# A pair's first product is copied to a second PSUM bank by ScalarE, and TensorE adds the second product there

## The chip, the cores and the metric

The kernel runs on one core of a Trainium2 chip. The metric is the device time of one execution in microseconds (us); a kernel is run several times, and the median is given. The hardware profiler records one execution, whose instructions make up the profile. TensorE does the matrix products into PSUM, a memory of eight banks of 128 x 512 fp32 numbers; VectorE and ScalarE read the banks and write to SBUF, the working memory; GpSimd (POOL) and SyncE (SP) mostly issue transfers here.

## The reference

Two layers of a block with two branches, on 512 tokens of width 1024, in fp32:

```python
h = rmsnorm(x, norm1_g[i])
z = h @ w_in[i] + b_in[i]              # q,k,v,o, gates of both branches
hm = mlstm_chunkwise(...)              # branch A, 4 heads, q and k through a causal conv
hr = retention_chunkwise(...)          # branch B, 4 heads
merged = sigmoid(gm) * (y_m @ w_bm[i]) + sigmoid(gr) * (y_r @ w_br[i])
x = x + merged @ w_out[i]
h2 = rmsnorm(x, norm2_g[i])
x = x + square(relu(h2 @ w_ff1[i] + b_ff1[i])) @ w_ff2[i] + b_ff2[i]
h3 = rmsnorm(x, norm3_g[i])
x = x + sigmoid(h3 @ w_pe_gate[i]) * (p[i] @ w_pe[i])
return rmsnorm(x, final_g)             # after both layers
```

The weights are square matrices of width 1024 or strips of it; the feed-forward is 4096 wide.

## The kernel before

**Precision.** A product in fp32 is made of three products of a shorter type: each operand is split into a high part, copied by ScalarE (L309), and a low part, the difference, made by VectorE (L310). TensorE then multiplies high by high, high by low and low by high into one bank. The weights are split as they arrive, into buffers that hold three blocks of each sort: w, w_A, w_B, w_C, w_D, w_t. A block of 128 x 1024 takes one instruction of each engine.

**Pairs.** A part of the products is made in units called PAIR, by a scheme of seven half-size products in place of eight (`run_pair`, L520). Each of the seven, P1 to P7, is 12 matmuls of 128 x 256: four row blocks by three precision terms. TensorE does them in the order P1, P5, then the P4 that the previous pair has left (`flush`), P6, P2, P3, P7. A pair uses three banks: P1, P6, P7 and P4 are summed in bank a, one on top of the other; P5 and P3 in bank c; P2 is alone in bank b. After every product a reader takes out what stands in its bank, and the next product on the same bank waits for that reader. So P6 waits for the reader of P1, P7 for that of P6, and P4 for that of P7. There are 75 pairs, 35 in the first layer and 40 in the second.

**Readers.** In `pair_tiles` (L597), used for the projections, the gates and the pairs of the first feed-forward product, ScalarE copies P1 out (L612) and VectorE adds P2 to it (L616). In `ff2` (L1524), the second feed-forward product (32 of the 75 pairs, tiles named l0o00 to l1o33), VectorE adds each product to x (L1530 where it is the first to touch x, L1532 elsewhere); there P1 and P2 go to the same quarter of x.

**What sets the order.** The program is written in one sequence, and a scheduler sorts the instructions of each engine from it by readiness and priority; the readers of `pair_tiles` are raised (`tc.high_priority(AHEAD)`). At run time each engine goes through its list in order and waits where something is not ready. A bank comes from a pool, `ps`, of eight; a tile that asks for one waits for the last reader of the tile that had it.

**The first head.** In the mLSTM the four column blocks of q and k (l0m0z0 to z3, `mm3`, L488 to L490) and the four token blocks of v (l0m0vp0 to vp3, L809 to L811) are made ahead of the norm's factor, which VectorE multiplies in when it reads z (L1040); z0 is the first that it reads. In the list before, TensorE takes vp0 to vp3 in turn for each block of weights.

Of the kernel before, what the change touches and what calls it, by code (L numbers as in the profile page):

```python
# [35 lines left out]
F32 = mybir.dt.float32  # L36
F32R = mybir.dt.float32r
AF = mybir.ActivationFunctionType
OP = mybir.AluOpType
# [3 lines left out]
P = 128  # L43
T = 512
# [7 lines left out]
S = 256  # L52
UN = 1024
LOOK = 2
AHEAD = 250
WARM = 13
# [23 lines left out]
def ff_order():  # L80

    seq = [("f", 0, p) for p in range(4)]
    for b in range(3):
        seq.append(("f", b + 1, 0))
        seq += [("o", b, p) for p in range(4)]
        seq += [("f", b + 1, p) for p in range(1, 4)]
    return seq, [("o", 3, p) for p in range(4)]
# [166 lines left out]
def build(ctx, tc, ins, out):  # L254
    nc = tc.nc
    ve, ac, gp, te = nc.vector, nc.scalar, nc.gpsimd, nc.tensor
# [3 lines left out]
    def pool(name, bufs, **kw):  # L260
        return ctx.enter_context(tc.tile_pool(name=name, bufs=bufs, **kw))
# [8 lines left out]
    wpool = pool("w", PIECES)  # L270
    bpool = pool("big", 1)
    opool = pool("one", 1)
    psum = pool("ps", 8, space=bass.MemoryType.PSUM)
    cur = {}

    xs_dram = tc.dram_tile([KT, P, T], F32, name="x_spill")
# [20 lines left out]
    ones = ones_r.bitcast(F32)  # L297
# [3 lines left out]

    def ps(name):
        return psum.tile([P, T], F32, name=name, tag="ps")

    def tmp(name, dt=F32):
        return cur["tmp"].tile([P, T], dt, name=name, tag="t", bufs=cur["ntmp"])
# [64 lines left out]
    def pace():  # L371
        if at["step"] < len(steps) and at["credit"] >= 0:
            step()
# [6 lines left out]
    def next_unit():  # L380
        n = at["unit"]
        at["unit"] += 1
        tick("FULL" if full(n) and units[n][0] == "PAIR" else units[n][0])
        return n
# [92 lines left out]
    def ready(k):  # L477
        while at["prep"] < min(len(order), k + 1):
            prep_next()

    def unit(kind):
        n = next_unit()
        assert units[n][0] == kind, (units[n], kind)
        ready(place[n, 0] + LOOK)
        return units[n], *pieces.pop((n, 0))
# [6 lines left out]
    def t8(act, name):  # L492

        _, wh, wl = unit("T8")
        o = ps(name)
        for k in range(KT):
            s = slice(k * P, (k + 1) * P)
            mm3(o, wh[:, s], wl[:, s], act[0][k], act[1][k], k == 0, k == KT - 1)
            if k == 3:
                flush()  # L500
            if k in (2, 5):
                pace()
        return o

    def acts(pl, name):
        hi, lo = [], []
        for k in range(KT):
            hi.append(pl.tile([P, T], F32R, name=f"{name}h{k}", tag="ah", bufs=KT))
            lo.append(pl.tile([P, T], F32R, name=f"{name}l{k}", tag="al", bufs=KT))
        return hi, lo  # L510
# [4 lines left out]
    def flush():  # L515

        while later:
            later.pop()()

    def run_pair(name, act, done):  # L520

        n = next_unit()
        assert units[n][0] == "PAIR", units[n]
        bank = {}

        def product(x):
            w, half, j = PRODUCTS[x]
            ready(place[n, "A"] + READY[x])
            wh, wl = [a[:, half * Q:(half + 1) * Q] for a in pieces[n, w]]
            b = {"P2": "b", "P5": "c", "P3": "c"}.get(x, "a")  # L530
            first = x in ("P1", "P2", "P5")
            if first:
                bank[b] = ps(f"{name}{b}")
            o = bank[b][:, 0:S]
            for k in range(4):
                s = slice(k * P, (k + 1) * P)
                h, l = act[k](j)
                f, e = first and k == 0, k == 3
                te.matmul(o, wh[:, s], h, start=f, stop=False, skip_group_check=True)
                te.matmul(o, wh[:, s], l, start=False, stop=False, skip_group_check=True)  # L540
                cur["mm"] = te.matmul(o, wl[:, s], h, start=False, stop=e, skip_group_check=True)  # L541
            done(x, o)
            pace()

        def last():
            product("P4")
            for w in PIECE:
                del pieces[n, w]

        product("P1")  # L550
        product("P5")
        flush()
        for x in ("P6", "P2", "P3", "P7"):
            product(x)
        later.append(last)
# [34 lines left out]
                then[x, u]()  # L590
            pace()

    def ahead():

        return tc.high_priority(AHEAD)

    def pair_tiles(name, act, consume, y=None, then=None):  # L597

        y = y or [tmp(f"{name}y{d}") for d in range(2)]
        a, b = slice(0, S), slice(S, T)  # L600

        def done(x, o):
            with ahead():
                evict(x, o)
            if then and x in then:
                then[x]()
            if x == "P4":
                consume(y)

        def evict(x, o):  # L610
            if x == "P1":
                ac.activation(y[0][:, b], o, AF.Copy)  # L612
            elif x == "P5":
                ac.activation(y[1][:, a], o, AF.Copy)
            elif x == "P2":
                ve.tensor_tensor(y[0][:, b], o, y[0][:, b], OP.add)  # L616
            elif x == "P6":
                ac.activation(y[1][:, b], o, AF.Copy)
            elif x == "P3":
                ve.tensor_tensor(y[1][:, b], o, y[1][:, b], OP.add)  # L620
            elif x == "P7":
                ve.tensor_tensor(y[1][:, a], o, y[1][:, a], OP.add)
            else:
                ac.activation(y[0][:, a], o, AF.Copy)

        run_pair(name, act, done)
# [142 lines left out]
    def bcol(i, n, k):  # L769
        o, _ = _B[n]  # L770
        return bvec(i, o + k)
# [187 lines left out]
    def big(name, dt):  # L959

        return [bpool.tile([P, T], dt, name=f"{name}{k}", tag="big", bufs=KT) for k in range(KT)]

    x = big("x0", F32)
# [2 lines left out]
    cur["tmp"], cur["ntmp"] = cur["low"], NTMP  # L966
    cur["room"] = range(room)
    n1 = Norm("l0n1", 0, "g1", acts(xa_pool, "l0n1"))
    warm = ps("warm")
    for _ in range(WARM):  # L970
        te.matmul(warm[:, 0:P], ones, ones, start=True, stop=True)
    nc.sync.dma_start(x[0], ins["xT"][0])
    fill_raws(2)
    nc.scalar.dma_start(bc[:, 0, 8:NK], ins["vecs"][0][:, 8:NK])
# [11 lines left out]
    for i in range(L):  # L986
# [34 lines left out]
        _, wi = unit("IF")  # L1021
        _, wh, wl = unit("T8")
        og = ps(f"l{i}if")
        oz = ps(f"l{i}m0z0")
        for k in range(KT):
            s = slice(k * P, (k + 1) * P)
            f, e = k == 0, k == KT - 1
# [281 lines left out]
        for d in range(4):  # L1309
            o = t8(xa, f"l{i}m0z{d}") if d else oz  # L1310
# [115 lines left out]
        for c in range(KT):  # L1426
# [6 lines left out]
            o = t8(yr, f"l{i}br1{c}")  # L1433
# [13 lines left out]
        if i == L - 1:  # L1447
            x_pool = phase("x", act_side)
            whole = x_pool.tile([P, KT, T], F32, name=f"l{i}x", tag="x")
            x = [whole[:, c, :] for c in range(KT)]  # L1450
        else:
            x = big(f"l{i}x", F32)
# [18 lines left out]
        for c in range(KT):  # L1471
            o = t8((mh, ml), f"l{i}wo{c}")
# [47 lines left out]
        def tile3(c):  # L1520
            n3.tile(c, x[c])

        def ff2(b, p):
            started = set()  # L1524

            def add(q, o, op):
                y = x[2 * p + q // 2][:, (q % 2) * S:(q % 2 + 1) * S]
                if b == 0 and q not in started:
                    started.add(q)
                    ve.scalar_tensor_tensor(y, y, bcol(i, "bf2", 2 * p + q // 2), o, OP.add, op)  # L1530
                else:
                    ve.tensor_tensor(y, y, o, op)  # L1532

            def done(x_, o):
                if x_ in ("P1", "P2"):
                    add(1, o, OP.add)
                elif x_ == "P5":
                    add(2, o, OP.subtract)
                elif x_ in ("P6", "P3"):
                    add(3, o, OP.subtract)  # L1540
                elif x_ == "P7":
                    add(2, o, OP.subtract)
                elif x_ == "P4":
                    add(0, o, OP.add)
                    if b == 3 and p == 3:
                        tile3(6)
                        tile3(7)
                if b == 3 and p and x_ in ("P6", "P7"):
                    tile3(2 * p - 2 + (x_ == "P7"))

            def parts(k):
                h, l = hid[b, k]
                return lambda j: (h[:, j * S:(j + 1) * S], l[:, j * S:(j + 1) * S])

            run_pair(f"l{i}o{b}{p}", [parts(k) for k in range(4)], done)

        first, rest = ff_order()
# [59 lines left out]
        for c in range(KT - LAST if last else KT):  # L1617
            o = t8(n3.act, f"l{i}pg{c}")
# [44 lines left out]
    for a, n in enumerate(nn):  # L1663
        for c in range(KT - LAST, KT):
            _, wh, wl = ws[c - KT + LAST]
            o = ps(f"pl{a}{c}")[:, :256]
# [141 lines left out]
```

## Time and profile before

| | |
|---|---|
| median of 3 runs | 2288.41 us (2288.2 to 2289.22) |
| the profiled execution | 2288.05 us |
| its span | 2286.3 us |
| matmuls | 13532 |
| TensorE busy | 2266.4 us |
| VectorE busy | 1761.6 us in 2722 instructions |
| ScalarE busy | 1265.9 us in 1835 instructions |
| granted TensorE clock | 0.998 |

Names in rows give the tile written, an arrow, and the tiles read. "L310 DVE" is an instruction of line 310 on VectorE, ACT is ScalarE, PE is TensorE. A timeline row gives the start in us from the span's start, the duration, and in brackets the idle time before it and who ended it. Tile numbers are left out: l0m0z stands for z0 to z3.

### The profile page before, as it was taken

What the parts mean: (1) busy time and instruction counts of PE and PEld (TensorE: products, weight loads), DVE (VectorE), ACT (ScalarE), POOL (GpSimd) and SP (SyncE); (2) the same over time, 40 slices, a digit from 0 to 9 for tenths busy, and PEclk for the clock granted to TensorE, in tenths of its full rate; (3) what the DMA queues carried; (4) which work ended last, traced back from release to release, by engine and by line L of the source; (5) the groups of instructions that cost most, each with busy time, mean ns of one, the idle gap of its engine ahead of it and who ended that gap; (6) DMA issues with size and microseconds to landing.
All of it is one profiled execution on the core that took longest, in us unless ns stands there. A gap on an engine that the chain in (4) does not pass through costs nothing.

```text
span 2286.3 us, 36395 instructions
## 1 busy us (share of the span) xinstructions
PE 2266.4 (99%) x13532; PEld 2011.6 (88%) x13532; DVE 1761.6 (77%) x2722; ACT 1265.9 (55%) x1835; POOL 610.0 (27%) x952
## 2 busy tenths in 40 slices
PE   9999999999999999999999999999999999999998
PEld 8888899888898899999888888988888888999997
DVE  7877777886677878778778787778867678787785
ACT  6766544654554546556557564445545446566564
POOL 3332222223124322223532332221231242111112
PEclk9999999999999999999999999999999999999999
DMA  6776887787789888888886768877876888888841
GB/s 214 191 193 175 245 231 220 217 234 213 230 239 267 218 229 233 236 247 221 219 224 182 197 179 249 238 215 225 227 221 213 247 265 218 248 235 229 233 162 56
DMA packets 187890, 499.33 MB, mean 218 GB/s; under 512 B 26352, under 2 KB 29808, under 8 KB 187712
## 3 DMA queue, kind: packets, MB, share of 16 engines
q0 software_dynamic: 57520, 188.53, 36.9%
q1 hardware_dynamic: 114496, 280.97, 36.3%
q10 hardware_dynamic: 15696, 27.50, 3.5%
q8 instruction: 106, 1.74, 0.3%
q14 instruction: 72, 0.59, 0.1%
HBM read 478.03 MB, written 194.51 MB: 294 GB/s over the span
## 4 chain that ended last, share of the span: by engine, by line
PE 87%; DVE 7%; ACT 2%; issue 2%; DMA 2%; POOL 0%; SPq 0%; DVEq 0%; ACTq 0%; POOLq 0%
PE l1br L488 1%; PE l0br L489 1%; PE l0br L488 1%; PE l1br L489 1%; PE l0br L490 1%; PE l1br L490 1%; PE l0f L488 1%; PE l0f L490 1%; PE l0f L489 1%; DVE w_B L310 1%; DVE w_C L310 1%; PE l1f L488 1%; PE l0pg L488 1%; PE l1f L490 1%; PE l1bm L488 1%
## 5 line engine op out<-in xcount | busy, mean ns | idle before, releaser
L309 ACT ACTIVATE w<-wr 128x1024 fp32r<-128x1024 f32 (+1 forms) x193 | 199.7, 1041 | 124.7 <-issue 28.5
L310 DVE TENSOR_TENSOR w<-wr,w 128x1024 fp32r<-128x1024 f32 (+1 forms) x193 | 234.1, 1216 | 43.7 <-ACT w L309 42.8
L309 ACT ACTIVATE w_B<-wr 128x1024 fp32r<-128x1024 f32 x123 | 130.4, 1060 | 148.8 <-PE l1bm L490 13.1
L310 DVE TENSOR_TENSOR w_B<-wr,w_B 128x1024 fp32r<-128x1024 f32 x123 | 150.2, 1222 | 54.3 <-ACT w_B L309 53.8
L309 ACT ACTIVATE w_C<-wr 128x1024 fp32r<-128x1024 f32 x75 | 79.3, 1058 | 65.0 <-issue 6.8
L310 DVE TENSOR_TENSOR w_C<-wr,w_C 128x1024 fp32r<-128x1024 f32 x75 | 92.5, 1233 | 25.6 <-ACT w_C L309 24.7
L310 DVE TENSOR_TENSOR w_A<-wr,w_A 128x1024 fp32r<-128x1024 f32 x75 | 91.7, 1223 | 13.7 <-ACT w_A L309 9.6
L309 ACT ACTIVATE w_A<-wr 128x1024 fp32r<-128x1024 f32 x75 | 79.1, 1054 | 41.2 <-DMA wr<-wpairs 4.4
L309 ACT ACTIVATE w_t<-wr 128x1024 fp32r<-128x1024 f32 x56 | 59.4, 1060 | 64.1 <-PE l1g2va L585 6.3
L309 ACT ACTIVATE w_D<-wr 128x512 fp32r<-128x512 f32 x75 | 47.3, 631 | 81.8 <-DVE wr L470 27.4
L310 DVE TENSOR_TENSOR w_t<-wr,w_t 128x1024 fp32r<-128x1024 f32 x56 | 68.3, 1222 | 21.3 <-ACT w_t L309 20.7
L488 PE MATMUL l0f<-l0n2h,w 128*128 128x512 f32 x176 | 68.7, 390 | 0.0
L489 PE MATMUL l0f<-l0n2l,w 128*128 128x512 f32 x176 | 68.6, 390 | 0.0
L490 PE MATMUL l0f<-l0n2h,w 128*128 128x512 f32 x176 | 68.5, 389 | 0.0
L310 DVE TENSOR_TENSOR w_D<-wr,w_D 128x512 fp32r<-128x512 f32 x75 | 51.7, 690 | 15.0 <-ACT w_D L309 14.5
L367 POOL DMA_DIRECT2D s30t<-wpairs x24 | 16.8, 701 | 92.3 <-PE l1o10a L541 9.2
L490 PEld LDWEIGHTS l0f<-l0n2h,w 128*128 128x128 f32 x176 | 33.0, 188 | 7.0
L488 PEld LDWEIGHTS l0f<-l0n2h,w 128*128 128x128 f32 x176 | 33.0, 188 | 6.6
L489 PEld LDWEIGHTS l0f<-l0n2l,w 128*128 128x128 f32 x176 | 33.0, 188 | 6.5
L488 PE MATMUL l1f<-l1n2h,w 128*128 128x512 f32 x96 | 37.6, 391 | 0.0
L489 PE MATMUL l1f<-l1n2l,w 128*128 128x512 f32 x96 | 37.4, 390 | 0.0
L490 PE MATMUL l1f<-l1n2h,w 128*128 128x512 f32 x96 | 37.4, 389 | 0.0
(5796 smaller groups left out, 9080.3 us busy)
## 6 DMA issues: line engine op xcount, KB each, us to landing
wr<-wstream SPq DMA_DIRECT2D x189, 512.0 KB, 4.8
wr<-wpairs SPq DMA_DIRECT2D x225, 256.0 KB, 4.0
wr<-wwide SPq DMA_DIRECT2D x48, 512.0 KB, 4.5
s3t<-wwide POOLq DMA_DIRECT2D x24, 256.0 KB, 4.7
s6t<-wwide POOLq DMA_DIRECT2D x24, 256.0 KB, 5.2
s18t<-wwide POOLq DMA_DIRECT2D x24, 256.0 KB, 5.5
s21t<-wwide POOLq DMA_DIRECT2D x24, 256.0 KB, 5.0
s24t<-wpairs POOLq DMA_DIRECT2D x24, 256.0 KB, 6.3
```

The source lines that it names most:

```text
L309: a = ac.activation(hi_ap, src, AF.Copy)
L310: return a, ve.tensor_sub(lo_ap, src, hi_ap.bitcast(F32))
L367: dma = gp.dma_start(piece(g, x, p, q), piece(g, MADE[x][a], p, q), max_dma_last_dim=4096, **kw)
L488: te.matmul(o, sh, mh, start=first, stop=False)
L489: te.matmul(o, sh, ml, start=False, stop=False)
L490: cur["mm"] = te.matmul(o, sl, mh, start=False, stop=last)
```

## The change

Each pair keeps its three banks, but b now comes from a pool of its own with one bank, `psb`, and the common pool `ps` has seven. When P1 is done, ScalarE copies bank a into bank b. P2 is then started without clearing, so that TensorE adds it onto the copy, and P2's reader takes out the sum: in `pair_tiles` a copy of ScalarE where VectorE's addition was, in `ff2` one addition to x where there were two. So a pair has one addition of VectorE less and one copy of ScalarE more; the number of matmuls is the same. The matmuls of the warm-up at the program's start write to the two halves of what P2 uses of the new bank, whose accumulation marks are set by that; no later matmul clears them.

```diff
-    psum = pool("ps", 8, space=bass.MemoryType.PSUM)
+    psum = pool("ps", 7, space=bass.MemoryType.PSUM)
+    psum_b = pool("psb", 1, space=bass.MemoryType.PSUM)
...
+    def seeded(name):
+
+        return psum_b.tile([P, T], F32, name=name, tag="psb")
...
     def run_pair(name, act, done):
...
-            first = x in ("P1", "P2", "P5")
+            first = x in ("P1", "P5")
             if first:
                 bank[b] = ps(f"{name}{b}")
...
-            done(x, o)
+            if x == "P1":
+                bank["b"] = seeded(f"{name}b")
+                with ahead():
+                    ac.activation(bank["b"][:, 0:S], o, AF.Copy)
+            else:
+                done(x, o)
             pace()
...
         def evict(x, o):
-            if x == "P1":
+            if x == "P2":
                 ac.activation(y[0][:, b], o, AF.Copy)
             elif x == "P5":
                 ac.activation(y[1][:, a], o, AF.Copy)
-            elif x == "P2":
-                ve.tensor_tensor(y[0][:, b], o, y[0][:, b], OP.add)
...
-    warm = ps("warm")
-    for _ in range(WARM):
-        te.matmul(warm[:, 0:P], ones, ones, start=True, stop=True)
+    warm = seeded("warm")
+    for k in range(WARM):
+        te.matmul(warm[:, k % 2 * P:k % 2 * P + P], ones, ones, start=k == 0, stop=True, skip_group_check=True)
...
             def done(x_, o):
-                if x_ in ("P1", "P2"):
+                if x_ == "P2":
                     add(1, o, OP.add)
```

The scheduler sorts the lists anew, so that instructions also stand elsewhere far from the pairs. Three places follow; line numbers of the changed kernel are five to eight higher.

TensorE at the first head of the first layer, before (vp2 and vp3 are the third and fourth token block of v; w5 is the first block of weights, w7 the third):

```order
L810 MATMUL l0m0vp2_618<-w5_0_447,l0n1h0_202 128x512
L811 MATMUL l0m0vp2_618<-w5_0_447,l0n1l0_203 128x512
L809 MATMUL l0m0vp3_619<-w5_0_447,l0n1h0_202 128x512
L810 MATMUL l0m0vp3_619<-w5_0_447,l0n1h0_202 128x512
L811 MATMUL l0m0vp3_619<-w5_0_447,l0n1l0_203 128x512
L809 MATMUL l0m0vp0_616<-w5_0_447,l0n1h1_204 128x512
```

and of the change, where vp3's first matmul stands:

```order
L817 MATMUL l0m0vp2_621<-w7_0_626,l0n1h4_213 128x512
L818 MATMUL l0m0vp2_621<-w7_0_626,l0n1h4_213 128x512
L819 MATMUL l0m0vp2_621<-w7_0_626,l0n1l4_214 128x512
L817 MATMUL l0m0vp3_622<-w5_0_450,l0n1h0_205 128x512
L818 MATMUL l0m0vp3_622<-w5_0_450,l0n1h0_205 128x512
L819 MATMUL l0m0vp3_622<-w5_0_450,l0n1l0_206 128x512
```

vp3 now begins only when vp0 to vp2 have gone through five of their eight row blocks: 45 matmuls behind vp0's first, where it was 9. In the second layer it is 50.

VectorE at the same place, before (l0gf to l0gc are the gates' rows, w_0 a block of weights that is split, l0m00z the read of z0):

```order
L913 SCALAR_TENSOR_TENSOR l0gf<-l0gf,l0gd 4x512
L310 TENSOR_TENSOR w_0_655<-wr_406,w_0_655 128x1024
L919 SCALAR_TENSOR_TENSOR l0glb<-ones_r,l0glf 4x128 x4
L921 SCALAR_TENSOR_TENSOR l0gm<-l0glf,l0gli 4x512
L937 TENSOR_TENSOR l0gc<-l0gli,l0glb 4x128
L923 TENSOR_TENSOR l0gr__522<-l0glb,l0gm 4x512
L937 TENSOR_TENSOR l0gc<-l0gli,l0glb 4x128 x3
L1040 TENSOR_TENSOR l0m00z<-l0m0z_317,l0n1rb 128x512
```

and of the change:

```order
L921 SCALAR_TENSOR_TENSOR l0gf<-l0gf,l0gd 4x512
L927 SCALAR_TENSOR_TENSOR l0glb<-ones_r,l0glf 4x128 x4
L929 SCALAR_TENSOR_TENSOR l0gm<-l0glf,l0gli 4x512
L945 TENSOR_TENSOR l0gc<-l0gli,l0glb 4x128
L931 TENSOR_TENSOR l0gr__525<-l0glb,l0gm 4x512
L945 TENSOR_TENSOR l0gc<-l0gli,l0glb 4x128 x3
L1048 TENSOR_TENSOR l0m00z<-l0m0z_320,l0n1rb 128x512
```

The split of a block of weights, one instruction, no longer stands ahead of the read of z0.

VectorE at the pair l0o10 of the second feed-forward product, before (l0o10a is the pair's bank a, the row with it is P1's addition):

```order
L1494 TENSOR_TENSOR l0f20st<-l0f_8929,l0n2rb 128x512
L310 TENSOR_TENSOR w_B<-wr_8838,w_B 128x1024
L1532 TENSOR_TENSOR l0x_7205<-l0x_7205,l0o10a 128x256
L631 TENSOR_TENSOR l0f20st<-l0f20st 128x512
L470 TENSOR_TENSOR wr_8838<-wr_8838 128x512
```

of the change, the same place on VectorE:

```order
L1502 TENSOR_TENSOR l0f20st<-l0f_8932,l0n2rb 128x512
L315 TENSOR_TENSOR w_B<-wr_8841,w_B 128x1024
L475 TENSOR_TENSOR wr_8841<-wr_8841 128x512
L639 TENSOR_TENSOR l0f20st<-l0f20st 128x512
L315 TENSOR_TENSOR l0hl_8861<-l0f20st,l0hh_8860 128x768
```

and on ScalarE, where L554 is the new copy of bank a to bank b:

```order
L314 ACTIVATE w_B<-wr_8841 128x1024
L554 ACTIVATE l0o10b<-l0o10a 128x256
L1503 ACTIVATE l0f20st<-l0f20st,bc 128x512
L1504 ACTIVATE l0f20st<-l0f20st 128x512
```

P1's addition is gone from VectorE, and the copy stands on ScalarE directly behind the high half of w_B.

More of the change, by code (lines that the diff above doesn't have):

```diff
@@ L518, in flush, with ahead @@
             later.pop()()
+    def ahead():
+        return tc.high_priority(AHEAD)
     def run_pair(name, act, done):
@@ L591, in run_wide @@
             pace()
-    def ahead():
-        return tc.high_priority(AHEAD)
     def pair_tiles(name, act, consume, y=None, then=None):
```

## The prediction

> **What bounds the kernel now.** I read the page first, then the waits of TensorE, then single sites in the timeline.
>
> ```profile
> span 2286.3 us, 36395 instructions
> PE 2266.4 (99%) x13532; PEld 2011.6 (88%) x13532; DVE 1761.6 (77%) x2722; ACT 1265.9 (55%) x1835; POOL 610.0 (27%) x952
> PE 87%; DVE 7%; ACT 2%; issue 2%; DMA 2%; POOL 0%; SPq 0%; DVEq 0%; ACTq 0%; POOLq 0%
> ```
>
> The span is TensorE's own work: it is busy 99%, and the chain that ended last lies on it for 87%. VectorE's 77% is cover as long as its result comes before TensorE asks for it. The number of matmuls doesn't change, so at best the change takes from the 2286.3 - 2266.4 = 19.9 us that TensorE idled. The next view says who ended that idle time; the columns are the wait, its releaser, us in total, times and longest. These are the rows inside the pairs.
>
> ```profile
> PE l1o20a L539 <- DVE l1x L1532: 1.2, 1, 1.2
> PE l1f10a L541 <- DVE w_B L310: 0.8, 1, 0.8
> PE l0o10a L539 <- DVE l0x L1532: 0.7, 1, 0.7
> PE l0o20a L539 <- DVE l0x L1532: 0.7, 1, 0.7
> PE l1o10a L540 <- DVE l1hl L310: 0.6, 1, 0.6
> PE l1o32a L539 <- DVE l1x L1532: 0.5, 1, 0.5
> PE l1o00a L539 <- DVE l1x L1532: 0.5, 1, 0.5
> ...
> PE l1o10a L539 <- ACT l1hh L309: 0.4, 1, 0.4
> ...
> PE l1o20a L540 <- DVE l1hl L310: 0.3, 1, 0.3
> PE l0o30a L541 <- DVE w_B L310: 0.3, 1, 0.3
> PE l1o30a L541 <- DVE w_B L310: 0.3, 1, 0.3
> PE l1o33a L539 <- DVE l1x L1532: 0.3, 1, 0.3
> PE l1bgm2a L541 <- DVE w_B L310: 0.3, 1, 0.3
> PE l0bgm2a L541 <- DVE w_B L310: 0.3, 1, 0.3
> ...
> PE l1f10a L539 <- ACT l1f10st L612: 0.2, 1, 0.2
> PE l1o10b L541 <- DVE w_B L310: 0.2, 1, 0.2
> PE l1o20b L541 <- DVE w_B L310: 0.2, 1, 0.2
> PE l0o00a L539 <- DVE l0x L1530: 0.2, 1, 0.2
> ```
>
> Eighteen waits. Seven are on an addition of VectorE that empties a bank (1.2 + 0.7 + 0.7 + 0.5 + 0.5 + 0.3 + 0.2 = 4.1 us), eleven on a weight or operand that is split late, or in one case copied out late by ScalarE (0.8 + 0.6 + 0.4, five of 0.3 and three of 0.2: 3.9 us). Together 8.0 us, 0.35% of the span. No row names a bank outside the pairs: with eight banks nothing waits for one.
>
> What one costs in full is seen at the first product P6 of l0o10.
>
> ```profile
> 895.60 1.22 DVE L310 TENSOR_TENSOR w_B<-wr,w_B 128x1024 fp32r<-128x1024 f32 x1
> 896.73 0.42 DVE L1532 TENSOR_TENSOR l0x<-l0x,l0o10a 128x256 f32<-128x256 f32 x1
> 895.10 0.28 PE L539 MATMUL l0o10c<-l0hh,w_A 128*128 128x256 f32 x1
> ...
> 896.35 0.28 PE L541 MATMUL l0o10c<-l0hh,w_A 128*128 128x256 f32 x1
> 897.29 0.36 PE L539 MATMUL l0o10a<-l0hh,w_B 128*128 128x256 f32 x1 [0.67 <-DVE l0x L1532]
> ```
>
> P5's twelve matmuls start at 895.10 to 896.35, 1.25 / 11 = 0.114 us apart, so P6 was due at 896.46 and came 0.83 us late: the idle 0.67 and 0.16 more. Eighteen waits so cost 8.0 + 18 x 0.16 = 10.9 us, the most that the listed ones can give back.
>
> **What it removes.** One addition of VectorE for each pair.
>
> ```profile
> L616 DVE TENSOR_TENSOR l0r0brqy<-l0r0brqb,l0r0brqy x1: 419/419/419, 310.2 to 310.2; 128x256 f32<-128x256 f32 x1
> L1532 DVE TENSOR_TENSOR l0x<-l0x,l0o10a x4: 414/416/417, 896.7 to 908.0; 128x256 f32<-128x256 f32 x4
> L612 ACT ACTIVATE l0r0brqy<-l0r0brqa x1: 384/384/384, 305.7 to 305.7; 128x256 f32<-128x256 f32 x1
> 816.00:856.00 40.00, 39.77 (x347) 39.36 (x346) 34.23 (x55) 17.80 (x22) 8.96 (x14) 1.00 0.85 244
> 2070.00:2108.00 38.00, 37.65 (x281) 35.53 (x280) 30.24 (x43) 26.91 (x39) 7.33 (x11) 1.00 0.81 226
> ```
>
> There are 75 pairs: 75 x 0.42 = 31.5 us less on VectorE, 75 x 0.384 = 28.8 us more on ScalarE. Both lie beside TensorE. The windows (PE, weight loads, VectorE, ScalarE, POOL) are a stretch of second feed-forward products and one of first: VectorE is busy 34.23 of 40 us and 30.24 of 38, ScalarE 17.80 and 26.91. The change moves work from the fuller engine to the emptier one. By site:
>
> - P6 behind P1's own addition (l0o10, l0o20, l0o00: 0.7, 0.7, 0.2). At l0o10 the addition goes and ScalarE's copy takes its place much earlier, since P1 ended 1.36 us before P5 did; but P6 also needs w_B's low half, which ends at 896.82. So it starts 0.42 earlier and not 0.82. Two at 0.42 and the short one whole with its 0.16: 1.2 us.
> - P4 behind P7's addition (l1o20, l1o32, l1o00, l1o33). An addition removed helps only where VectorE ran without a gap from it to P7's. At l1o20 it did not:
>
> ```profile
> 2115.12 1.23 DVE L310 TENSOR_TENSOR w_C<-wr,w_C 128x1024 fp32r<-128x1024 f32 x1 [1.37 <-ACT w_C L309]
> 2118.07 0.41 DVE L1532 TENSOR_TENSOR l1x<-l1x,l1o20a 128x256 f32<-128x256 f32 x1
> 2114.03 1.06 ACT L309 ACTIVATE w_C<-wr 128x1024 fp32r<-128x1024 f32 x1 [1.57 <-DMA wr<-s28t]
> ```
>
>   VectorE stood 1.37 us for a weight that ScalarE, and before it a transfer, delivered late: nothing gained. For the other three between 0 and 3 x 0.42 = 1.3; I take 0.5.
> - Eleven late splits: between 0 and 11 x 0.42 = 4.6 us, bounded by their 3.9 + 11 x 0.16 = 5.7. A split waits for ScalarE's half first and that engine gets a copy more, so less than half: 1.9.
> - Stalls too short for the list: all rows of the view come to 12.4 of the 19.9 us, which leaves 7.5 in the whole span; the pairs hold 75 x 84 matmuls x 0.114 = 718 us of it, a third, so 2.3 us, of which I take half: 1.2.
>
> Gain: 1.2 + 0.5 + 1.9 + 1.2 = 4.8 us, between 0 and 13.2 (10.9 + 2.3).
>
> **What it adds.** ScalarE copies bank a to bank b right after P1, and P2 waits for it. Between P1's end and P2 stand P5, the late P4 and P6, 3 x 12 x 0.114 = 4.1 us; P6 comes 2.7 us behind P1. No row of the trace shows a copy from PSUM to PSUM: the nearest is L612, PSUM to SBUF, 0.384; what lies ahead of it on ScalarE is a split of 1.06 at most. So it is done between 0.4 and 0.384 + 1.06 = 1.44 us behind P1, inside 2.7 even if it took twice L612's time: nothing. P2's eviction by ScalarE instead of VectorE frees the bank before the next P1 ends, three products (4.1 us) later. The warm-up moves to the new bank and costs what it did.
>
> **What it moves.** The common banks go from 8 to 7. At the first head of the mLSTM the kernel holds exactly eight: z0 to z3, all kept until the norm of the layer is known, and vp0 to vp3. With seven, vp3 must wait until VectorE has read z0 (L1040). The built order answers by running vp0 to vp2 ahead: vp3's first matmul is 45 matmuls behind vp0's first in layer 0 and 50 in layer 1, where it was 9.
>
> ```profile
> L809 PE MATMUL l0m0vp<-w,l0n1h x32: 389/389/389, 34.6 to 55.7; 128*128 128x512 f32 x32
> 41.33 1.23 DVE L310 TENSOR_TENSOR w<-wr,w 128x1024 fp32r<-128x1024 f32 x1 [0.21 <-ACT w L309]
> 42.47 1.35 DVE L919 TENSOR_TENSOR_SCAN l0glb<-ones_r,l0glf 4x128 f32<-4x128 f32 x4
> 46.66 0.67 DVE L1040 TENSOR_TENSOR l0m00z<-l0m0z,l0n1rb 128x512 f32<-128x512 f32 x1
> 41.32 0.63 ACT L915 ACTIVATE l0glf<-l0gf 4x512 f32<-4x512 f32 x1
> L809 PE MATMUL l1m0vp<-w,l1n1h x32: 389/389/389, 1167.4 to 1188.4; 128*128 128x512 f32 x32
> 1180.62 0.67 DVE L1040 TENSOR_TENSOR l1m00z<-l1m0z,l1n1rb 128x512 f32<-128x512 f32 x1
> ```
>
> The first and last of 93 steps give 21.1 / 93 = 0.227 us a matmul. vp3 is due at 34.6 + 45 x 0.227 = 44.8. VectorE ends z0 at 47.33; the split at 41.33 now stands behind it, so the scan may start when ScalarE's L915 ends, 41.95 and not 42.47, and z0 ends at 46.8: a wait of 2.0 us. In layer 1, 1167.4 + 50 x 0.227 = 1178.75 against 1181.29 - 0.5 = 1180.8: 2.0 us. Sum 4.0, with 0.16 each to start again 4.3. Unhelped by the shift it is 5.3. The lower bound is 2: a TensorE that is late by 2 us finds later results ready and may win half back.
>
> One other place loses its slack: the third head's z0 now takes the bank of l0m0ot.
>
> ```profile
> L488 PE MATMUL l0m2z<-l0xnh,w x32: 389/389/396, 119.2 to 140.3; 128*128 128x512 f32 x32
> L883 DVE SCALAR_TENSOR_TENSOR l0m0o0g<-l0m0ot,bc,l0m0o0g x1: 748/748/748, 119.2 to 119.2; 128x512 f32<-128x512 f32 x1
> ```
>
> The read ends 119.95, the matmul was due at 119.2: 0.75 us, or nothing if TensorE comes there 2 us later than before and VectorE does not. I take 0.4, and 0.5 for the other rows of VectorE that stand elsewhere (0 to 2).
>
> By the Trainium skill, page "Perfetto Trace Analysis", section "Matmul Optimizations", all eight PSUM banks should be in use for the most parallelism; a bank set aside for P1's copy goes against it, and the first head, where eight are held at once, is where this trace agrees. The page gives no price; the 4.3 us above are from rows alone.
>
> Sum: -4.8 + 4.3 + 0.4 + 0.5 = +0.4 us on this execution. Its own time is 2288.05, its span and 1.75 us around it; that lies 0.36 below the median of 2288.41. So 2288.8 us.
>
> **The rivals.**
>
> *VectorE was the bound of the pairs* (chance 0.25). For it: all but two of the eighteen waits name VectorE, and it is 86% busy in the second products. Against it: P6 needs w_B too, and l1o20 hangs on a transfer. If the listed waits go entirely and the banks cost the 4.3: 2288.4 - 10.9 + 4.3 = 2281.8 us. The Trainium skill points this way on the same page, "Optimizing Scalar/DVE Operations": work for a saturated VectorE may be given to ScalarE. Whether 86% counts as saturated no row here says.
>
> *Seven banks cost more than VectorE gives* (0.20, the other side). The mechanism is the wait of a first matmul for the reader of a bank. For it: eight were held, and the largest new wait is 2.0 us twice. If VectorE's shift does not help, 5.3 us; if in the six later heads the wait of l0m2z0 comes in full, 6 x 0.9 = 5.4; with half of the gain, 2288.4 + 5.3 + 5.4 - 2.4 = 2296.7 us. It decides once the bank waits exceed the gain by 4.6 us. Against it: in the later heads z0 is read soon, as the norm is known.
>
> *ScalarE's queue* (0.05, slower too). A copy behind a weight whose transfer is late, as at 2114.03 (1.57 us), would hold P6. Six such of the 32 pairs of the second products: 2288.8 + 6 x 1.57 = 2298.2 us. Against it: those waits fall behind P5, and the copy stands ahead of them.
>
> **How the numbers follow.** 0.2% of the time, 4.6 us, is what a measurement here can tell from no change. The forecast, a gain and a loss that cancel, has 0.48, its own range 2284.5 to 2293. Faster is the first rival, with 0.02 from the forecast's edge: 0.27. Slower are the other two: 0.25. Same 0.48. For 8 in 10 the range takes in the first rival and reaches below it by part of the short stalls (2280), and the second above (2297).
>
> **What would show it.** VectorE's count falls by 75 to 2647 and its busy time by some 31 us; ScalarE's rises by 75 and some 29. TensorE's waits should hold two new rows near 2 us, l0m0vp and l1m0vp at L817 on VectorE's L1048, and none of P6 on an addition; l1o20 at L547 stays near 1.2. The list's splits should shrink by less than half. I am wrong if vp3 does not wait, if pairs still wait as much as 8.0 us, or if ScalarE's copy appears as a releaser of P2 or P6.

## The result, and the profile after

Timed in turn with the kernel before, 22 times each, the change took 2293.24 us (2289.66 to 2295.86) and the kernel before 2289.51 us (2286.99 to 2292.56). The ratio is 1.0015, with a 95% interval of 1.0009 to 1.0021: 3.4 us slower, between 2.1 and 4.8. That is a small loss, inside the 0.2% that the prediction called no change. The ratios in this document leave out two executions of later runs that took 2497.15 and 4626.91 us.

The page of the change: the span, then busy time, share and number of instructions by engine.

```profile
span 2293.4 us, 36383 instructions
PE 2270.1 (99%) x13532; PEld 2014.0 (88%) x13532; DVE 1738.6 (76%) x2647; ACT 1288.7 (56%) x1910; POOL 603.6 (26%) x952
```

The change does what it says: VectorE has 75 instructions less and is busy 1761.6 - 1738.6 = 23.0 us less, ScalarE has 75 more and is busy 22.8 us more, the matmuls are as many. The two profiled executions lie 7.1 us apart in span, twice what the medians do: that of the change took 2295.13 us, 1.9 above its median, and that of before 2288.05 us, 1.5 below its own.

TensorE's waits in the change, the longest and those inside pairs that the text uses:

```profile
PE l1m0vp L817 <- DVE l1m00z L1048: 2.0, 1, 2.0
PE l0m0vp L817 <- DVE l0m00z L1048: 1.8, 1, 1.8
PE l0r0brqa L548 <- DVE l0r0brqy L630: 1.3, 1, 1.3
...
PE l1bgm L495 <- DVE w L315: 0.9, 1, 0.9
...
PE l0o10c L548 <- DVE l0x L1540: 0.4, 1, 0.4
...
PE l0o10a L550 <- DVE w_B L315: 0.4, 1, 0.4
PE l0o20a L550 <- DVE w_B L315: 0.3, 1, 0.3
```

The two waits of vp3 stand on top. Two more long ones were not there before: l0r0brqa (the late P4 of the first retention pair) and l1bgm. Shorter new ones stand at P3 of l0o00, l0o10, l0o20 and l1o20 (0.4 us each). Of the list of before, l1o20a, l1f10a, l1o32a and l1o00a are gone, and so is P6's wait on an addition at l0o10 and l0o20. All rows of this view inside pairs come to 5.8 us, where the prediction's eighteen came to 8.0.

**The first head.** Timeline of the change, VectorE's read of z0 and TensorE's first matmul of vp3, for the first layer and the second.

```profile
46.65 0.67 DVE L1048 TENSOR_TENSOR l0m00z<-l0m0z,l0n1rb 128x512 f32<-128x512 f32 x1
47.37 0.50 PE L817 MATMUL l0m0vp<-w,l0n1h 128*128 128x512 f32 x1 [1.80 <-DVE l0m00z L1048]
1187.26 0.67 DVE L1048 TENSOR_TENSOR l1m00z<-l1m0z,l1n1rb 128x512 f32<-128x512 f32 x1
1187.99 0.50 PE L817 MATMUL l1m0vp<-w,l1n1h 128*128 128x512 f32 x1 [2.03 <-DVE l1m00z L1048]
```

In both, TensorE starts 0.05 to 0.06 us after z0's reader ends (47.32 and 1187.93). Against the usual step of 0.227 us, the start is 1.96 us late in the first layer and 2.19 in the second, 4.15 together.

**The new wait at l0r0brq.** Timeline of the kernel before, two instructions of VectorE; then of the change, VectorE and TensorE's P4.

```profile
312.07 0.42 DVE L620 TENSOR_TENSOR l0r0brqy<-l0r0brqc,l0r0brqy 128x256 f32<-128x256 f32 x1
314.07 0.69 DVE L467 TENSOR_TENSOR wr<-wr,wr 128x512 f32<-128x512 f32 x1 [1.59 <-DMA wr<-wpairs]
```

```profile
316.73 0.69 DVE L472 TENSOR_TENSOR wr<-wr,wr 128x512 f32<-128x512 f32 x1 [3.62 <-DMA wr<-wpairs]
317.34 0.42 DVE L628 TENSOR_TENSOR l0r0brqy<-l0r0brqc,l0r0brqy 128x256 f32<-128x256 f32 x1
317.67 1.22 DVE L315 TENSOR_TENSOR w_C<-wr,w_C 128x1024 fp32r<-128x1024 f32 x1
318.80 0.42 DVE L630 TENSOR_TENSOR l0r0brqy<-l0r0brqa,l0r0brqy 128x256 f32<-128x256 f32 x1
319.27 0.39 PE L548 MATMUL l0r0brqa<-l0xnh,w_D 128*128 128x256 f32 x1 [1.30 <-DVE l0r0brqy L630]
```

L472 adds two blocks of weights and needs a transfer. VectorE stands 3.62 us for it, and behind it in the queue stand P3's addition (L628), the split of w_C and P7's addition (L630), for which P4 waits. In the list before, P3's addition (L620 there) and the split stood ahead of that instruction (L467 there) and were done while the transfer was under way. Here they take 317.34 to 318.80, 1.46 us, and TensorE is late by as much.

**A pair where the relief went nowhere.** Timeline at l0o10, before: P5's addition on VectorE and TensorE's P3, which is 0.29 us late.

```profile
900.49 0.41 DVE L1532 TENSOR_TENSOR l0x<-l0x,l0o10c 128x256 f32<-128x256 f32 x1
900.96 0.39 PE L539 MATMUL l0o10c<-l0hh,w_C 128*128 128x256 f32 x1
```

Of the change: w_B's split and P5's addition on VectorE, then the starts of TensorE that were late (in P6, and in P3).

```profile
900.92 1.22 DVE L315 TENSOR_TENSOR w_B<-wr,w_B 128x1024 fp32r<-128x1024 f32 x1
905.52 0.42 DVE L1540 TENSOR_TENSOR l0x<-l0x,l0o10c 128x256 f32<-128x256 f32 x1
902.19 0.39 PE L550 MATMUL l0o10a<-l0hh,w_B 128*128 128x256 f32 x1 [0.35 <-DVE w_B L315]
906.00 0.39 PE L548 MATMUL l0o10c<-l0hh,w_C 128*128 128x256 f32 x1 [0.41 <-DVE l0x L1540]
```

P1's addition is gone, and P6 now waits for w_B alone: late by 0.52 us in place of 0.83. But P3 needs P5's addition, and that came no sooner: 905.52 - 900.49 = 5.03 us later than before, where TensorE's P5 had begun 4.99 us later. P3's wait grew from 0.29 to 0.58 us by the starts of TensorE. What the one wait gave, the next took.

**A pair where a wait went, perhaps not by the change.** At l1o20, P4 before:

```profile
2118.54 0.39 PE L539 MATMUL l1o20a<-l1hh,w_D 128*128 128x256 f32 x1 [1.17 <-DVE l1x L1532]
```

and in the change, ScalarE's w_C, P7's addition on VectorE, and P4:

```profile
2120.42 1.06 ACT L314 ACTIVATE w_C<-wr 128x1024 fp32r<-128x1024 f32 x1 [0.34 <-DMA wr<-s28t]
2123.86 0.41 DVE L1540 TENSOR_TENSOR l1x<-l1x,l1o20a 128x256 f32<-128x256 f32 x1
2124.56 0.28 PE L548 MATMUL l1o20a<-l1hh,w_D 128*128 128x256 f32 x1
```

The transfer held ScalarE 0.34 us where it had held it 1.57, P7's addition ended at 2124.27, and P4, late by 1.33 us before, started 0.12 us behind the matmul ahead of it, so not late at all. The copies need not be the reason: e1_seven and e8_seven_again below are one kernel without a copy, and there P4 is 1.32 us late in the first execution and on time in the second, where the transfer held ScalarE 0.34 us too.

```profile
2123.58 1.06 ACT L310 ACTIVATE w_C<-wr 128x1024 fp32r<-128x1024 f32 x1 [0.34 <-DMA wr<-s28t]
```

### The profile page after: what moved, and what is told of

Same layout as the page of the kernel before. It is cut to its first block, busy times and chain, and to the rows that moved or that the text cites. A ratio compares the mean times of both kernels' runs of the same rounds, so it can differ in the third digit from the quotient of the medians.

```text
span 2293.4 us, 36383 instructions
## 1 busy us (share of the span) xinstructions
PE 2270.1 (99%) x13532; PEld 2014.0 (88%) x13532; DVE 1738.6 (76%) x2647; ACT 1288.7 (56%) x1910; POOL 603.6 (26%) x952
## 5 line engine op out<-in xcount | busy, mean ns | idle before, releaser
L314 ACT ACTIVATE w_t<-wr 128x1024 fp32r<-128x1024 f32 x56 | 59.3, 1061 | 63.1 <-PE l0g2va L599 6.3
```

Of the source, the lines that this page charges most:

```text
L314: a = ac.activation(hi_ap, src, AF.Copy)
```

## The experiments

My theory was that the bank costs, at vp3 of the first heads, and that VectorE's relief inside the pairs repays a part. The rival was that the bank is hidden and the copies, or the order that comes with them, cost. Every kernel was timed in turn with the kernel before on the same chip: e1, e2, e3 and e5 together on one chip, the other four together on another.

| run | what it is | median, us | kernel before beside it, us | ratio, 95% interval |
|---|---|---|---|---|
| e1_seven | before, seven common banks | 2298.29 | 2288.15 | 1.0039 (1.0025 to 1.0053) |
| e2_vp3 | change, vp3 in the pairs' bank | 2285.83 | 2288.15 | 0.9989 (0.9980 to 0.9998) |
| e3_ff2 | e2_vp3, copy in the second products only | 2284.62 | 2288.15 | 0.9983 (0.9974 to 0.9992) |
| e5_again | the change again | 2294.50 | 2288.15 | 1.0027 (1.0017 to 1.0036) |
| e6_seven_vp3 | e1_seven, vp3 in the eighth bank | 2289.72 | 2288.77 | 1.0003 (0.9994 to 1.0012) |
| e4_tiles | e2_vp3, copy outside the second products only | 2290.92 | 2288.77 | 1.0008 (0.9999 to 1.0017) |
| e7_again | the change a third time | 2293.52 (one run) | 2288.77 | |
| e8_seven_again | e1_seven a second time | 2297.95 (one run) | 2288.77 | |

**e1_seven: the bank taken away, nothing else.**

```diff
 the kernel before
-    psum = pool("ps", 8, space=bass.MemoryType.PSUM)
+    psum = pool("ps", 7, space=bass.MemoryType.PSUM)
+    psum_b = pool("psb", 1, space=bass.MemoryType.PSUM)
...
-    warm = ps("warm")
+    warm = psum_b.tile([P, T], F32, name="warm", tag="psb")
```

> The kernel before with one thing changed: the common pool has seven banks, and the eighth holds the warm-up alone. No copy, all 75 additions of VectorE are back. Theory A (the bank is what costs: vp3 of each layer's first head waits for z0, and the change's relief of VectorE pays part of it back): TensorE waits about 2 us twice for l0m00z and l1m00z, nothing is paid back, so 4 to 6 us above the kernel before, which is as slow as the change or slower. Theory B (the bank is hidden, the copy and the new order inside the pairs cost): no wait of vp3, within 1 us of the kernel before.

It took 0.39% more than the kernel before, 8.9 us (5.7 to 12.1): more than the change, and more than I had expected. Its TensorE's waits:

```profile
PE l1m0vp L810 <- DVE l1m00z L1041: 2.0, 1, 2.0
PE l0m0vp L810 <- DVE l0m00z L1041: 1.8, 1, 1.8
...
PE l1o20a L540 <- DVE l1x L1533: 1.2, 1, 1.2
...
PE l0o10a L540 <- DVE l0x L1533: 0.7, 1, 0.7
```

Both waits of vp3 are there without a single copy, and the waits of the pairs are nearly those of before. So the loss comes with the bank, and the copies seem to make it smaller: 1.0039 here and 1.0027 for the change timed beside it, some 2.7 us, though the two intervals meet.

**e2_vp3: the change, with eight banks for the first head.** vp3 is put into the bank of the pairs, which no pair uses at that time.

```diff
 the change
-        o = [ps(f"{nm}vp{j}") for j in range(NT)]
+        o = [(seeded if j == 3 and nm.endswith("m0") else ps)(f"{nm}vp{j}") for j in range(NT)]
```

> The change with one thing undone: vp3 of each layer's first head takes the pairs' own bank, which is idle there, so that eight banks serve the first head as before. Theory A: both waits of vp3 go and 4.2 us with them, the late split of l1bgm (0.9 us) perhaps too; the wait of l0r0brq's P4 (1.3 us) stays, as its order on VectorE is the change's. So 3.5 to 5 us below the change, within 1.5 us of the kernel before or a little under it. Theory B: as slow as the change, 3 to 4 us above the kernel before.

It took 0.11% less than the kernel before, 2.5 us (0.5 to 4.6), and 2294.50 - 2285.83 = 8.7 us less than the change timed beside it, well above the 3.5 to 5 expected. Neither vp3 nor l1bgm is among its waits any more; that of l0r0brq stays, and so do the short ones at l0o10:

```profile
PE l0r0brqa L548 <- DVE l0r0brqy L630: 0.9, 1, 0.9
...
PE l0o10c L548 <- DVE l0x L1540: 0.4, 1, 0.4
...
PE l0o10a L550 <- DVE w_B L315: 0.3, 1, 0.3
```

One tile's place turns the change from a loss into a small gain. The rival, that the copies cost more than they give, falls.

**e6_seven_vp3: seven banks, and vp3 in the eighth; no copy.**

```diff
 e1_seven
-        o = [ps(f"{nm}vp{j}") for j in range(NT)]
+        o = [psum_b.tile([P, T], F32, name=f"{nm}vp{j}", tag="psb") if j == 3 and nm.endswith("m0") else ps(f"{nm}vp{j}") for j in range(NT)]
```

> The kernel before with seven common banks, and the eighth holds only the warm-up and vp3 of each layer's first head; no copy. If the bank costs at vp3 alone, and the other new waits of the run with seven banks come from the order that follows it, this is level with the kernel before, within 1.5 us. If seven banks cost elsewhere too, it stands 3 us or more above.

Level with the kernel before: 1.0003 (0.9994 to 1.0012). By the traces its engines do their work in the order of before but for some 8 of VectorE's 2722 instructions, 6 of ScalarE's and 20 matmuls, so little but the bank differs. Seven banks show no cost, to within 2.7 us, but at vp3 and through what follows from it. Unplaced, the bank costs 1.0039 - 1.0003 = 0.36%, 8.2 us here, and 8.7 us in the change. The pairs' copies are worth 0.9989 - 1.0003 = -0.14%, 3.2 us. These two differences are across runs on two chips, with intervals of some 2 to 3 us each way, so the 3.2 us could be anything from near nothing to 6.

**e3_ff2 and e4_tiles: the copy in one sort of pair.** Both are e2_vp3 with a parameter that leaves P1 and P2 as they were before, in the pairs of `pair_tiles` or in those of `ff2`.

```diff
 e2_vp3
-    def run_pair(name, act, done):
+    def run_pair(name, act, done, own=True):
...
-            first = x in ("P1", "P5")
+            first = x in ("P1", "P5") or not own and x == "P2"
...
-            if x == "P1":
+            if own and x == "P1":
```

> As the run with vp3 in the pairs' own bank, and the copy is made only in the pairs of the second feed-forward product (32 of 75); the other 43 take P1 and P2 out as before. Theory A: the wait of l0r0brq's P4 goes too, since VectorE's order there is that of before, and the waits that the change took away in the second feed-forward products (l1o00, l1o20, l1o32, l1f10 partly) stay away: 3 to 6 us below the kernel before if the gain lies in the second products, about level with it if it lies in the other 43. Theory B (copies cost in the pairs): slower than the kernel before by half of what the change is.

> The change only in the 43 pairs outside the second feed-forward product, with vp3 in the pairs' own bank; the 32 pairs of the second products add P1 and P2 apart, as before. If the gain lies in the second products alone: the wait of l0r0brq's P4 (0.9 to 1.3 us) is paid, l1f10's wait for w_B gets shorter (0.8), and the rest is nothing: 0 to 2 us above the kernel before. If the gain is spread over all pairs, as half of each late split: 1 to 2 us below it.

Only in the second products: 0.17% below the kernel before, 3.9 us (1.8 to 5.9). Only in the others: 0.08% above it, 1.8 us, which is not told from nothing (0.9999 to 1.0017). The two intervals do not meet: the gain lies in the 32 pairs of the second products, where the reader removed from VectorE is one of two additions on the same numbers. The traces narrow this down. From the first matmul of the second layer's second products to the last, the five profiles with the copy there took 3.8 to 6.8 us less than the kernel before, and the four others between 1.7 more and 2.3 less; in the first layer's, none of the nine is more than 1.0 us below it. Between the first head and the first layer's second products, the five profiles with the copy in the other 43 pairs took 2.1 to 2.6 us more, mostly at l0r0brq, and the others 0.1 to 1.3 us more. The longest waits in the pairs of e3_ff2:

```profile
PE l1f10a L550 <- DVE w_B L315: 0.6, 1, 0.6
...
PE l1o10a L549 <- DVE l1hl L315: 0.6, 1, 0.6
```

and of e4_tiles:

```profile
PE l0r0brqa L548 <- DVE l0r0brqy L630: 1.2, 1, 1.2
```

l0r0brq does not wait in e3_ff2, whose order on VectorE there is that of before, and does in e4_tiles. It is not the order alone, though: e6_seven_vp3, with the order of before, waits there too, for its transfer came late (2.42 us in place of 1.59).

```profile
315.02 0.69 DVE L468 TENSOR_TENSOR wr<-wr,wr 128x512 f32<-128x512 f32 x1 [2.42 <-DMA wr<-wpairs]
```

e3_ff2 is the fastest of all that were run. It is not told apart from e2_vp3 (0.9974 to 0.9992 against 0.9980 to 0.9998).

**e5_again, e7_again, e8_seven_again: the same kernels again.**

> The change once more, nothing altered. In its profile 2958 matmuls of 128x256 start 115 to 119 ns after the one before, in the profile of before 1527, and most others 113 to 114: whole stretches keep the longer step from one wait to another. Theory A (chance: how a wait happens to end decides which step TensorE keeps until the next wait): the stretches lie elsewhere, and their count differs by hundreds, while the waits of vp3 and l0r0brq come again at the same length. Theory B (the kernel's order decides): the same stretches, the count within 5%.

> The change a third time, for the two waits of vp3 and for what follows them. In six such waits so far (three profiles) two were followed by some 3.4 us in which a matmul of 512 columns took 427 ns and not 227, at a granted clock near 0.54 in that stretch. If that is chance, either wait may show it or not, the length stays 3.4 us and the price 1.6 to 1.8 us; if it hangs on the kernel's order, this profile is like the first one, with none.

> The run with seven banks alone once more, for the same question: its first profile had the slow matmuls after the wait of the second layer and none after that of the first. Chance: it may come out the other way. Order: the same again.

The waits of vp3 came again in each at 1.8 and 2.0 us, and that of l0r0brq at 1.1 and 1.7 us in the two further profiles of the change. The slow matmuls behind the waits came out as chance, and the longer step for the most part; both are told in the last section. As a second measurement of the change, e5_again gives 1.0027 (1.0017 to 1.0036), 6.2 us, where the first gave 1.0015 (1.0009 to 1.0021): it is slower in both, by a size that is known to a few us only.

## Why the prediction was right, and where it was wrong

The sum said +0.4 us with a gain and a loss that cancel; measured was +3.4 (2.1 to 4.8). The sign of the forecast was too close to nothing to mean much, and the time lies in the range, a little above the forecast's own. That it came out so near is in part luck: by the runs the gain is about 3 us and not 4.8, and the loss about 8 and not 5.2 (4.3 + 0.4 + 0.5), which makes some +5 us, between the 3.4 and the 6.2 of the two comparisons. The mechanism on the losing side was right, and its price was too small.

- **The wait of vp3** was put at 2.0 us a layer and 0.16 to start again: measured 1.96 and 2.19. The two-step reading (eight banks held at once, then due time against the reader's end) held, by the place, the engine named and the length.
- **What follows from it** is the term that was too small. The prediction let TensorE, being late, win half back as the lower bound, and gave 0.5 us to all other rows. The runs show the contrary: 8.2 us in all for the bank without copies, 8.7 with them. Of this, 4.15 are the waits. In five of ten of them the clock then fell for 3.4 us, 1.6 us each, so 1.6 us for the two on average. In the five profiles with this wait l1bgm was late by 0.3 to 1.1 us and l0m0s by 0 to 2.0 (on average 0.7 and 0.8); neither is late where vp3 has a bank. That comes to about 7 us. As a check, from the first layer's first projections to the end of l0m0s, and from the second layer's first matmul to the end of l1m0s, those five profiles took 6.6 to 9.7 us more than the kernel before, 8.0 on average, and the four with vp3 placed 0.1 to 1.2. So nearly the whole loss lies at the two first heads.
- **The third head's z0** (0.4 us) did not wait at all: TensorE came there at 121.92, 2.7 us later than before, and the reader of its bank had ended at 121.08. Here the lateness did cover a wait.
- **The gain in the pairs** was put at 4.8 us and measures about 3 (3.2 by e2_vp3 against e6_seven_vp3, 2.7 by e5_again against e1_seven). The mis-sized terms: P6 at l0o10, l0o20 and l0o00 gave 0.3 us each, and P3 of the same pair lost it again, since P5's addition stands in the same VectorE queue; the prediction priced the wait removed and not the wait next in that queue. Its 0.42 for one P6 was also more than its rows allow: P1's addition ended at 896.73 + 0.42 = 897.15, 0.33 us behind w_B's split. For l1o20's P4 it predicted nothing, and the wait of 1.33 us went with the transfer, which it had taken as fixed. P4 of l1o00, 0.61 us late in the four profiles with no copy at all, was late by 0.30 at most in the six others. The splits' 1.9 us were about right: their rows come to 2.2 us in the change where the list of before had 3.9 (with the two on ScalarE). l1f10 is late by 0.4 to 0.9 us in all five profiles without the copy in those 43 pairs and in none of the five with it. The 1.2 us for short stalls were not measured apart.
- **VectorE's relief** was counted as 75 x 0.42 = 31.5 us and is 23.0, 0.31 us for each addition, and ScalarE's copies cost 0.30 each and not 0.384: in the rows, instructions that follow one another closely overlap (at l0r0brq, L628 lasts until 317.76 and the next begins at 317.67), and busy time counts the overlap once.
- **The copy itself** hid nearly as predicted. The prediction's sign against it, a P6 released by the copy, occurs once, at l0gr0: TensorE starts 0.29 us late there, and it had waited as long before for ScalarE's P1.
- **l0r0brq's P4**, late by 1.3 to 1.9 us in the three profiles of the change, was missed. The front of this document says that instructions stand elsewhere far from the pairs; I had priced only the places where a bank was involved, and an instruction that waits for a transfer had moved ahead of the addition that P4 needs.

Of the rivals, the second one (seven banks cost more than VectorE gives) is nearest to what happened: its mechanism decided the sign, at the first head alone. Its other term, the six later heads, did not come. The first one, VectorE as the bound of the pairs, holds for some of the pairs of the second products, as e3_ff2 shows, at about a third of its price.

## What to carry to other kernels

Before a bank is set aside, find the place where all are held at once: there the first matmul waits for the oldest reader, and a single tile that may use the reserved bank while it stands idle can undo the cost (8.7 us against a gain of 3 here). Less work on an engine that TensorE waits for paid here only where the next result in that engine's queue came earlier too, so follow the queue to the next wait before counting a gain. A new order moves instructions that wait for transfers; look for one that now stands ahead of a result that TensorE needs. And before a vanished wait is put down to a change, look whether a second execution of a kernel without the change still has it.

## What the runs showed of the hardware that was not expected

**A wait of 2 us can cost the clock.** In e7_again, TensorE's matmuls after the second layer's wait, and windows of the same stretch (PE, weight loads, VectorE, ScalarE, POOL, then the granted clock):

```profile
1188.49 0.50 PE L817 MATMUL l1m0vp<-w,l1n1h 128*128 128x512 f32 x1 [2.03 <-DVE l1m00z L1048]
1188.83 0.39 PE L818 MATMUL l1m0vp<-w,l1n1h 128*128 128x512 f32 x1
...
1190.22 0.63 PE L817 MATMUL l1m0vp<-w,l1n1h 128*128 128x512 f32 x1
1190.65 0.63 PE L818 MATMUL l1m0vp<-w,l1n1h 128*128 128x512 f32 x1
...
1193.17 0.40 PE L818 MATMUL l1m0vp<-w,l1n1h 128*128 128x512 f32 x1
...
1189.90:1193.30 3.40, 3.40 (x10) 2.68 (x9) 3.40 (x7) 2.04 (x3) 2.06 (x3) 0.53 0.62 99
1193.30:1196.70 3.40, 3.40 (x22) 2.61 (x20) 3.08 (x5) 3.37 (x5) 2.65 (x4) 1.00 0.94 172
```

For 3.4 us the granted clock is 0.53 in the window and a matmul of 512 columns takes 1190.65 - 1190.22 = 0.43 us and not 0.227; eight of them cost 8 x 0.2 = 1.6 us. By the clock's records in the traces it began 0.1 to 1.5 us after TensorE had started again. It followed five of the ten waits of vp3: none of two in the first profile of the change, one of two in e5_again, e7_again and e1_seven, both in e8_seven_again. In the profiles without that wait (before, e2_vp3, e3_ff2, e4_tiles, e6_seven_vp3) it is not seen at the first heads, and it did not follow l0r0brq's wait in any. In e1_seven it came once more, at l1o10, where two waits stand one behind the other (starts 1.1 and 0.9 us late). So the same kernel pays it or not from one execution to the next. The Trainium skill, page "TensorE: Matmul & The Clock Gate", section "What's actually happening", has the clock halved after an idle window of about 3.4 us that runs freely and is not reset when a kernel starts. The length of the slow stretch and its chance agree with that; the idle time does not, for 2.0 us were enough here, and the measurement decides.

**Several steps of the matmul.** Windows of 18 us inside the pairs of the second products; the count behind PE is of matmuls. Before, then the change, then the change again:

```profile
994.00:1012.00 18.00, 18.00 (x161) 18.00 (x160) 13.83 (x23) 7.07 (x8) 3.89 (x6) 1.00 0.90 257
```

```profile
999.00:1017.00 18.00, 18.00 (x156) 18.00 (x155) 12.95 (x21) 8.14 (x10) 3.90 (x6) 1.00 0.88 247
```

```profile
1001.00:1019.00 18.00, 18.00 (x161) 18.00 (x161) 13.94 (x22) 7.22 (x10) 3.92 (x6) 1.00 0.85 250
```

At full clock and without a wait, TensorE does 161 or 156 of them in the same time. In the trace the starts are 0.1133 us apart in one stretch and 0.1167 in another, and a stretch goes on from one wait to the next, here for 355 matmuls, over four pairs. A third step occurs too: in e7_again 234 matmuls from 1061 us on start 0.120 us apart.

```profile
1062.00:1080.00 18.00, 18.00 (x152) 18.00 (x151) 15.18 (x22) 9.71 (x14) 6.97 (x9) 1.00 0.91 256
```

The step of 0.1167 was taken 1527 times in the profile of before, and 2958, 1820 and 1310 times in the three of the change; at 0.0034 us each, 5.2, 10.1, 6.2 and 4.5 us. Four stretches of some 157 matmuls (near 370, 530, 1500 and 1670 us) have it in nine of the ten profiles; the other long ones, where the counts differ, stand at other places from one execution of the change to the next, so there it is chance. The first two figures account for 4.9 of the 7.1 us by which the two profiled executions lay apart. It can also be one reason why repeated runs of one kernel differ by up to 6 us. What decides the step was not found.
